# Attention scores: the keys' low parts as two products of 64 rows, and transpositions taken in pairs

## The chip, the cores and the metric

The kernel runs on one core of a Trainium2 chip. The metric is the device time of one execution in microseconds (us). A profile is one execution recorded by the hardware profiler; its instructions stand at microseconds from the start of the span.

## What is computed

One layer of an encoder on 1024 tokens of width 1024: a norm and a projection, three mixers, a gated sum of the three, and a layer of 16 experts. The change lies in the third mixer, attention with 8 query heads of 64 columns on 2 key and value heads:

```python
def block(qb):
    s = jnp.einsum('bkgqd,bksd->bkgqs', qb, k_t).astype(jnp.float32)
    pr = jax.nn.softmax(s, axis=-1).astype(dt)
    return jnp.einsum('bkgqs,bksd->bkgqd', pr, v_t)
```

Queries and keys are normed and rotated before that, and everything is float32.

## The kernel before

TensorE (PE) multiplies in a rounded format, so every operand is split into a high part (rounded) and a low part (what the rounding left), and a product is summed from two or three products of parts. PE's order in attention is written out by hand, ScalarE (ACT), VectorE (DVE), GpSimd (POOL) and SyncE (SP, which issues most DMAs) are ordered by a scheduler that places an instruction where its own model of time says it can start. Tiles come from pools with a fixed number of buffers, and a pool that opens takes over room of one that has closed; its first writers then wait for the last users of that room.

`attention(g)` (L897) stands between the recurrent mixer (`gates_and_chain`, lines up to L894) and `mixers_to_experts` (L1041), whose first part, `phase3` (L1077), multiplies the three mixers' outputs with their branch weights. It goes like this:

- Keys (L906 to L915): for each of the 2 key heads a high part `kh` and a low part `kl`. The head's 64 rows stand twice in the 128 partitions, so that the same keys meet whatever lies in either half of a query tile.
- Queries, `queries(b)` (L927 to L937), for two heads at a time: the high part of a head's 64 rows goes to one half `a` of the partitions of a tile, the low part to the other half `o`. One product with 128 rows then sums (high + low) times the keys. ACT makes the high part, DVE (b = 0, 1) or POOL (b = 2, 3) the low one.
- Scores, `scores(u, t)` (L944): attention is cut into 16 units (a head and half of the tokens), a unit into 4 tiles of 128 queries. A tile's scores against 1024 keys are 4 products of 128 rows by 512 columns (L954 with `kh`, L955 with `kl`, for either half of the keys), 64 tiles in all. DVE takes the row's maximum (`mx`, L958), ACT the exponential with its sum (`P`, L961).
- `turned(u, kt)` (L966): the exponentials of 128 keys are turned by 4 transpositions on PE (L971) into one PSUM tile `pT` (3 buffers); ACT writes the high part `ph` (L980), DVE the low part `pl` (L981). The ninth turn of a unit (kt = 8) turns the reciprocal sums, read by L975 alone.
- `weighted(u, kt, part)` (L987): two products with the values (L995 with `ph`, L997 with `pl`) summed over the 8 key blocks in one PSUM tile `po` (1 buffer). After the eighth, ACT and DVE read it into `yc` (L1003), POOL multiplies by the reciprocals (L1004), and after every fourth unit POOL's queue stores `yc` (2 buffers) to DRAM (`d_yc`, L1008).

The order of PE is a list of slots, nine to a unit: the turn kt of unit u in slot 9u + kt, its products two slots later (`PO_LAG`, one more for the first), four scores to a unit, two slots apart. It is sorted by slot, and within a slot turns come first, then scores, then products.

`phase3` begins with `branch(0, ...)` (L1092): its left operands are the pooling mixer's output `d_yb`, four loads of 512 KB (`yraw`, 2 buffers, L1125), each split by ACT and DVE (L1083, L1084), and multiplied on PE (L263 to L265).

Of the kernel before, what the change touches and what calls it, by code (L numbers as in the profile page):

```python
# [9 lines left out]
F32 = mybir.dt.float32  # L10
F32R = mybir.dt.float32r
# [9 lines left out]
S = 1024  # L21
# [9 lines left out]
SC_LEAD, SC_STEP, MX_LAG, EX_LAG, PO_LAG, PO_EXTRA, Q_LEAD, P_BUFS, PH_BUFS = 11, 2, 0, 1, 2, 1, 16, 13, 5  # L31
# [865 lines left out]
def attention(g):  # L897
    nc, tc = g.nc, g.tc
    with ExitStack() as es:
        psa = es.enter_context(tc.tile_pool(name="psa", bufs=3, space=PSUM, reuse_waits="tile"))  # L900
        pso = es.enter_context(tc.tile_pool(name="pso", bufs=1, space=PSUM, reuse_waits="tile"))
        pss = es.enter_context(tc.tile_pool(name="pss", bufs=2, space=PSUM, reuse_waits="tile"))


        kh, kl = [], []
        for kv in range(2):  # L906

            k = g.W.tile("w_raw")
            for h in range(2):
                nc.sync.dma_start(k[h * 64:(h + 1) * 64], g.d_qk[4, kv * 64:(kv + 1) * 64])  # L910
            th, tl = g.tile4k(S, F32R), g.tile4k(S, F32R)
            nc.scalar.activation(th, k, AF.Copy)
            nc.vector.tensor_tensor(tl, k, th.bitcast(F32), op=ALU.subtract)
            kh.append(th)
            kl.append(tl)  # L915

        vr = g.tile4k()
        nc.sync.dma_start(vr, g.d_qk[5])
        vr = vr.rearrange("p (t h v) -> p t h v", t=8, h=2)
        vv = [g.tile4k(S, F32R).rearrange("p (t a v) -> p t a v", t=8, a=2) for _ in range(2)]  # L920
        for kv in range(2):
            nc.scalar.activation(vv[kv][:, :, 0], vr[:, :, kv], AF.Copy)
            nc.vector.tensor_tensor(vv[kv][:, :, 1], vr[:, :, kv], vv[kv].bitcast(F32)[:, :, 0], op=ALU.subtract)

        QS = {}

        def queries(b):  # L927
            eng = getattr(nc, ENG_Q[b])
            q = g.W.tile("w_raw")
            nc.sync.dma_start(q, g.d_qk[b])  # L930
            for h in range(2):
                a = slice(h * 64, h * 64 + 64)
                o = slice(64 - h * 64, 128 - h * 64)
                t = g.W.tile(("w_hi", "w_lo")[h])
                nc.scalar.activation(t[a], q[a], AF.Copy)
                eng.tensor_tensor(t[o], q[a], t.bitcast(F32)[a], op=ALU.subtract)
                QS[2 * b + h] = t  # L937

        atb = es.enter_context(tc.tile_pool(name="atb", bufs=1, reuse_waits="tile"))

        UNITS = [(h, half) for h in range(8) for half in range(2)]
        P, PO, YC = {}, {}, {}

        def scores(u, t):  # L944

            h, half = UNITS[u]
            kv, q = h // 4, QS[h]
            if t == 0:
                P[u] = [], atb.tile([128, 4], F32, name="smx", bufs=4)
            qs = slice(half * 512 + t * 128, half * 512 + (t + 1) * 128)  # L950
            p = pss.tile([128, S], F32, name="sc", tag="sc")
            for n in range(2):
                ks = slice(n * 512, (n + 1) * 512)
                nc.tensor.matmul(p[:, ks], q[:, qs], kh[kv][:, ks], start=True, stop=False)  # L954
                nc.tensor.matmul(p[:, ks], q[:, qs], kl[kv][:, ks], start=False, stop=True)  # L955
            mx = atb.tile([128, 1], F32, name="mx", bufs=14)
            yield
            nc.vector.tensor_reduce(mx, p, op=ALU.max, axis=AX.X, negate=True)  # L958
            yield
            pt = atb.tile([128, S], F32, name="P", bufs=P_BUFS)  # L960
            nc.scalar.activation(pt, p, AF.Exp, bias=mx, accum_out=P[u][1][:, t:t + 1])  # L961
            P[u][0].append(pt)
            if t == 3:
                nc.vector.reciprocal(P[u][1], P[u][1])

        def turned(u, kt):  # L966

            p = psa.tile([128, 512], F32, name="pT", tag="sa")
            for t in range(4):
                a = P[u][0][t][:, kt * 128:(kt + 1) * 128] if kt < 8 else P[u][1][:, t:t + 1].to_broadcast([128, 128])  # L970
                nc.tensor.transpose(p[:, t * 128:(t + 1) * 128], a, g.ident)  # L971
            if kt == 8:
                rb = atb.tile([128, 512], F32, name="rb", bufs=2)
                r = head(u)
                nc.scalar.activation(rb[r], p[r], AF.Copy)  # L975
                P.pop(u)
                return rb[r]
            ph = atb.tile([128, 512], F32R, name="ph", bufs=PH_BUFS)
            pl = atb.tile([128, 512], F32R, name="pl", bufs=PH_BUFS)
            nc.scalar.activation(ph, p, AF.Copy)  # L980
            nc.vector.tensor_tensor(pl, p, ph.bitcast(F32), op=ALU.subtract)  # L981
            return ph, pl

        def head(u):
            return slice(UNITS[u][0] % 2 * 64, UNITS[u][0] % 2 * 64 + 64)

        def weighted(u, kt, part):  # L987

            h, half = UNITS[u]
            kv = h // 4  # L990
            if kt == 0:
                PO[u] = pso.tile([128, 512], F32, name="po", tag="po")
            po = PO[u]
            if kt < 8:
                nc.tensor.matmul(po, vv[kv][:, kt].rearrange("p a v -> p (a v)"), part[0], start=(kt == 0), stop=False,  # L995
                                 skip_group_check=True)
                nc.tensor.matmul(po[0:64], vv[kv][:, kt, 0], part[1], start=False, stop=(kt == 7), skip_group_check=True)  # L997
                return
            if u % 4 == 0:
                YC[0] = atb.tile([128, S], F32, name="yc", bufs=2)  # L1000
            yc = YC[0]
            y = yc[head(u), half * 512:(half + 1) * 512]
            last = [nc.scalar.activation(y, po[64:128], AF.Copy), nc.vector.tensor_add(y, y, po[0:64])]  # L1003
            nc.gpsimd.tensor_mul(y, y, part)  # L1004
            if u == W_AFTER:
                g.marks = [i.ins for i in last]
            if u % 4 == 3:
                nc.gpsimd.dma_start(g.d_yc[h // 2], yc)  # L1008

        E = mybir.EngineType  # L1010
        with ExitStack() as em:
            if ATT_MANUAL:
                em.enter_context(tc.manual_schedule(engines={getattr(E, e) for e in ATT_MANUAL}))
            nu = len(UNITS)

            todo = []
            for u in range(nu):
                for t in range(4):
                    s = u * 9 + t * SC_STEP - SC_LEAD
                    st = scores(u, t)  # L1020
                    todo += [(s, 2, st), (s + MX_LAG, 3, st), (s + EX_LAG, 4, st)]
                for kt in range(9):
                    i = u * 9 + kt
                    todo.append((i, 1, ("T", u, kt)))
                    todo.append((i + PO_LAG + (PO_EXTRA if kt == 0 else 0), 5, ("O", u, kt)))
            for b in range(4):
                todo.append((b * 36 - SC_LEAD - Q_LEAD, 0, b))
            todo.sort(key=lambda x: x[:2])
            parts = {}
            for i, k, x in todo:  # L1030
                if k == 0:
                    queries(x)
                elif k in (2, 3, 4):
                    next(x, None)
                elif k == 1:
                    parts[x[1:]] = turned(*x[1:])
                else:
                    weighted(*x[1:], parts.pop(x[1:]))
# [620 lines left out]
def hybrid_trunk_kernel(ctx: ExitStack, tc: tile.TileContext, names, *args):  # L1659
# [34 lines left out]
    if True:  # L1694
        with ExitStack() as ea:
            g.early = ea.enter_context(tc.tile_pool(name="early", bufs=1, reuse_waits="tile"))
            g.Dt = g.early.tile([64, 2, 8, NCH], F32, name="Dt")
            tp = ea.enter_context(tc.tile_pool(name="t4", bufs=1, reuse_waits="tile"))
            g.tile4k = lambda n=S, dt=F32: tp.tile([128, 1056], dt, name="tmp", tag="tmp", bufs=N_TMP)[:, :n]
            g.W = Weights(g, ea.enter_context(tc.tile_pool(name="wst", bufs=1, reuse_waits="tile")), W_RAW, 2)  # L1700
            phase1(g)
            attention(g)
        mixers_to_experts(g)
# [43 lines left out]
```

## Time and profile before

| | us |
|---|---|
| three runs, median (lowest to highest) | 2044.52 (2040.13 to 2051.64) |
| profiled execution, its time | 2044.28 |
| its span, first to last instruction | 2042.0 |
| attention, first score on PE to last product on PE | 895.5 to 1090.5 |

The profile gives each engine's busy time, a timeline of its instructions with what ended an idle time ahead of them, waits by pair of instructions, and for DMAs the issue and, for POOL's queue, the landing. A matmul's shape stands as rows*columns of the weights, so `128*128` is a full one, `64*128` one of 64 rows and `128*64` one of 64 columns. A matmul's recorded length overlaps the next one, so it is the distance of starts that tells what one costs PE. "issue" names an idle time that nothing in the profile explains.

### The profile page before, as it was taken

What the parts mean: (1) busy time and instruction counts of PE and PEld (TensorE: products, weight loads), DVE (VectorE), ACT (ScalarE), POOL (GpSimd) and SP (SyncE); (2) the same over time, 40 slices, a digit from 0 to 9 for tenths busy, and PEclk for the clock granted to TensorE, in tenths of its full rate; (3) what the DMA queues carried; (4) which work ended last, traced back from release to release, by engine and by line L of the source; (5) the groups of instructions that cost most, each with busy time, mean ns of one, the idle gap of its engine ahead of it and who ended that gap; (6) DMA issues with size and microseconds to landing.
All of it is one profiled execution on the core that took longest, in us unless ns stands there. A gap on an engine that the chain in (4) does not pass through costs nothing. (4 is left out here: it accounts for less than half of the span.)

```text
span 2042.0 us, 30594 instructions
## 1 busy us (share of the span) xinstructions
PE 1895.8 (93%) x11324; PEld 1531.2 (75%) x11324; DVE 1439.5 (70%) x2265; ACT 1042.8 (51%) x1539; POOL 566.1 (28%) x668
## 2 busy tenths in 40 slices
PE   6999999999989999989998989996779999999994
PEld 5878878778868888867776768874568888777883
DVE  6464465755165456668987893668969999888896
ACT  4454345531213321248885221334658888777784
POOL 2211112463156344302111575435211010100111
PEclk9999989999989999999998999997989999999997
DMA  5225353584299999920004644367879999995994
GB/s 158 62 73 138 100 149 95 152 196 111 86 189 171 167 207 196 201 104 32 11 12 159 220 132 164 144 220 285 310 261 382 395 387 400 389 374 182 342 385 171
DMA packets 394185, 403.80 MB, mean 198 GB/s; under 512 B 235111, under 2 KB 313525, under 8 KB 394037
## 3 DMA queue, kind: packets, MB, share of 16 engines
q1 hardware_dynamic: 385252, 373.00, 59.2%
q0 software_dynamic: 8784, 28.86, 5.2%
q8 instruction: 89, 1.46, 0.3%
q14 instruction: 60, 0.48, 0.1%
HBM read 325.73 MB, written 76.06 MB: 197 GB/s over the span
## 5 line engine op out<-in xcount | busy, mean ns | idle before, releaser
L263 PE MATMUL mm<-hn_hi,w_hi 128*128 128x512 f32 x592 | 234.5, 396 | 1.4 <-ACT w_hi L257 1.4
L264 PE MATMUL mm<-hn_lo,w_hi 128*128 128x512 f32 x592 | 235.3, 397 | 0.0
L265 PE MATMUL mm<-hn_hi,w_lo 128*128 128x512 f32 x592 | 233.5, 395 | 0.0
L258 DVE TENSOR_TENSOR w_lo<-w_raw,w_hi 128x1024 fp32r<-128x1024 f32 x56 | 76.1, 1358 | 122.6 <-ACT w_hi L257 122.6
L263 PEld LDWEIGHTS mm<-hn_hi,w_hi 128*128 128x128 f32 x592 | 112.0, 189 | 27.4 <-issue 3.2
L1482 DVE TENSOR_TENSOR lo<-wh,hi 128x1024 fp32r<-128x1024 f32 x103 | 123.2, 1220 | 10.9 <-ACT hi L1473 9.9
L264 PEld LDWEIGHTS mm<-hn_lo,w_hi 128*128 128x128 f32 x592 | 112.0, 189 | 24.8 <-issue 2.6
L265 PEld LDWEIGHTS mm<-hn_hi,w_lo 128*128 128x128 f32 x592 | 112.2, 190 | 24.3 <-issue 1.2
L1482 DVE TENSOR_TENSOR lo<-wl,hi 128x1024 fp32r<-128x1024 f32 x102 | 122.1, 1225 | 9.7 <-ACT hi L1473 8.7
L257 ACT ACTIVATE w_hi<-w_raw 128x1024 fp32r<-128x1024 f32 x56 | 59.1, 1057 | 131.2 <-PE mm L264 99.7
L1473 ACT ACTIVATE hi<-wh 128x1024 fp32r<-128x1024 f32 x104 | 109.3, 1060 | 32.8 <-PE py L265 16.6
L1473 ACT ACTIVATE hi<-wl 128x1024 fp32r<-128x1024 f32 x104 | 107.6, 1057 | 22.4 <-PE pg L265 10.1
L263 PE MATMUL pg<-hi,xgh 128*128 128x512 f32 x256 | 104.2, 407 | 7.7 <-ACT xgh L1502 7.7
L826 ACT ACTIVATE sv<-pu 32x128 f32<-32x128 f32 x128 | 33.8, 269 | 148.1 <-DVE sv L828 123.1
L832 PEld LDWEIGHTS pf<-sv,ot 128*96 128x96 f32 x1024 | 98.2, 172 | 10.5 <-DVE sv L828 4.2
L265 PE MATMUL pg<-hi,xgl 128*128 128x512 f32 x256 | 102.6, 401 | 3.3 <-DVE xgl L1503 3.2
L264 PE MATMUL pu<-lo,xgh 128*128 128x512 f32 x256 | 102.1, 399 | 1.6 <-POOL lo L1480 1.5
L264 PE MATMUL pg<-lo,xgh 128*128 128x512 f32 x256 | 103.0, 402 | 0.5 <-POOL lo L1480 0.5
L832 PE MATMUL pf<-sv,ot 128*96 128x64 f32 x1024 | 99.3, 256 | 3.2 <-DVE sv L828 2.9
L263 PE MATMUL pu<-hi,xgh 128*128 128x512 f32 x256 | 100.8, 394 | 1.5 <-DVE hid L1523 1.5
L264 PE MATMUL py<-lo,hidh 128*128 128x512 f32 x240 | 96.4, 402 | 5.9 <-DVE lo L1482 5.6
L265 PE MATMUL pu<-hi,xgl 128*128 128x512 f32 x256 | 100.0, 391 | 0.0
(422 smaller groups left out, 5147.5 us busy)
## 6 DMA issues: line engine op xcount, KB each, us to landing
w_raw<-in_w_in_dram SPq DMA_DIRECT2D x49, 512.0 KB
wh<-in_exp_up_dram SPq DMA_DIRECT2D x23, 1024.0 KB
wl<-in_exp_up_dram SPq DMA_DIRECT2D x22, 1024.0 KB
wl<-in_exp_down_dram SPq DMA_DIRECT2D x20, 1024.0 KB
wh<-in_exp_down_dram SPq DMA_DIRECT2D x20, 1024.0 KB
mg<-in_exp_gate_dram SPq DMA_DIRECT2D x19, 1024.0 KB
yr<-in_exp_up_dram SPq DMA_DIRECT2D x14, 1024.0 KB
yr<-in_exp_gate_dram SPq DMA_DIRECT2D x13, 1024.0 KB
```

Source lines behind the costliest of these rows:

```text
L257: nc.scalar.activation(hi, raw, AF.Copy)
L258: nc.vector.tensor_tensor(lo, raw, hi.bitcast(F32), op=ALU.subtract)
L263: nc.tensor.matmul(out, ah, bh, start=start, stop=False)
L264: nc.tensor.matmul(out, ah, bl, start=False, stop=False)
L265: nc.tensor.matmul(out, al, bh, start=False, stop=stop)
L826: nc.scalar.activation(sv[96:128, q::4, :], pu[r], AF.Copy)
L832: nc.tensor.matmul(pf[0:96, q, :], ot[:, q, 0:96], sv[:, q, :], start=True, stop=True)
L1473: nc.scalar.activation(hi, raw[:, j], AF.Copy)
L1482: nc.vector.tensor_tensor(lo, raw[:, j], hi.bitcast(F32), op=ALU.subtract)
```

## The change

The products with the keys' low parts take 64 rows where they took 128: for the first 512 keys the rows `a`, with the query's high part that lies there, for the other 512 keys the rows `o`, with a copy `q2` of that high part, made by POOL. The product of low part with low part is left out. Two turns are put into one even slot, one behind the other, and the products with values follow in pairs.

```diff
@@ queries(b), in the loop over the two heads
                 nc.scalar.activation(t[a], q[a], AF.Copy)
                 eng.tensor_tensor(t[o], q[a], t.bitcast(F32)[a], op=ALU.subtract)
-                QS[2 * b + h] = t
+
+                t2 = atb.tile([128, S], F32R, name="q2", bufs=4)
+                nc.gpsimd.tensor_copy(t2[o], t.bitcast(F32)[a])
+                QS[2 * b + h] = t, t2, a, o
@@ scores(u, t)
             for n in range(2):
                 ks = slice(n * 512, (n + 1) * 512)
                 nc.tensor.matmul(p[:, ks], q[:, qs], kh[kv][:, ks], start=True, stop=False)
-                nc.tensor.matmul(p[:, ks], q[:, qs], kl[kv][:, ks], start=False, stop=True)
+
+            nc.tensor.matmul(p[:, :512], q[a, qs], kl[kv][a, :512], start=False, stop=True)
+            nc.tensor.matmul(p[:, 512:], q2[o, qs], kl[kv][o, 512:], start=False, stop=True)
@@ the list of slots
+            at = 0
...
                 for kt in range(9):
                     i = u * 9 + kt
-                    todo.append((i, 1, ("T", u, kt)))
-                    todo.append((i + PO_LAG + (PO_EXTRA if kt == 0 else 0), 5, ("O", u, kt)))
+
+                    todo.append((i // 2 * 2, 1, ("T", u, kt)))
+                    at = max(at, i // 2 * 2 + PO_LAG + (PO_EXTRA if kt == 0 else 0))
+                    todo.append((at, 5, ("O", u, kt)))
```

In the changed kernel the lines are L958 (scores, high), L960 and L961 (the two of 64 rows), L977 (transpositions), L1001 and L1003 (products with values), L939 (the copy), L1134 (`yraw`), L1111 (`sg`), L1014 (the store of `yc`).

PE, in the middle of attention. `sc` are scores, `pT` transpositions, `po` products with values. Before:

```order
L954 MATMUL sc<-tmp,w_hi 128x512
L955 MATMUL sc<-tmp,w_hi 128x512
L954 MATMUL sc<-tmp,w_hi 128x512
L955 MATMUL sc<-tmp,w_hi 128x512
L995 MATMUL po<-ph,tmp 128x512
L997 MATMUL po<-pl,tmp 64x512
L971 MATMUL pT<-ident,P 128x128 x8
```

After, in the same stretch:

```order
L958 MATMUL sc<-tmp,w_hi 128x512 x2
L960 MATMUL sc<-tmp,w_hi 128x512
L961 MATMUL sc<-tmp,q_9132 128x512
L1001 MATMUL po<-ph,tmp 128x512
L1003 MATMUL po<-pl,tmp 64x512
L1001 MATMUL po<-ph,tmp 128x512
L1003 MATMUL po<-pl,tmp 64x512
L977 MATMUL pT<-ident,P 128x128 x8
```

The count of matmuls is the same; the two with low keys now stand side by side at the end of a score, and behind the 64 scores stand 37 times a product with values, 23 times transpositions and 4 times the next score (at the very start, where scores run ahead).

SP, from the last store of the stage ahead of attention into `phase3`; the names in brackets are the semaphores that an issue waits for, by engine or DMA queue (DMASW are POOL's queues). Before:

```order
L725 DMA d_sig<-gate 128x512 [waits Activation_49]
L1125 DMA yraw<-d_yb 128x1024 [waits DMASW5_49,DMASW4_49,DMASW6_49,DMASW3_49,DMASW7_49,DMASW2_49,DMAHW5_49,DMASW1_49,DMASW0_49]
L1125 DMA yraw<-d_yb 128x1024 [waits DMASW7_49,DMAHW6_49,DMASW1_49,PE_49]
L1102 DMA sg<-d_sig 128x1024 [waits DMAHW7_49,DMAHW4_49]
L1102 DMA sg<-d_sig 128x1024 [waits DMAHW0_49]
L1102 DMA sg<-d_sig 128x1024 [waits DMAHW1_49]
L240 DMA w_raw<-in_w_branch_pool_dram 128x4x256 [waits DMAHW2_49,DVE_49]
L240 DMA w_raw<-in_w_branch_pool_dram 128x4x256 [waits DMAHW3_49,DVE_49]
L1135 DMA lnw<-in_rwkv_ln_w_dram 128x512 [waits PE_49]
```

After:

```order
L240 DMA w_raw<-in_w_branch_pool_dram 128x4x256 [waits DMAHW5_49,DMAHW1_49,DVE_49]
L240 DMA w_raw<-in_w_branch_pool_dram 128x4x256 [waits DMAHW6_49,DMAHW2_49,DVE_49]
L1134 DMA yraw<-d_yb 128x1024 [waits DMASW4_49,DMASW5_49,DMASW3_49,DMASW6_49,DMASW2_49,DMASW7_49,DMASW1_49,DMAHW7_49,DMASW0_49,Pool_49]
L1134 DMA yraw<-d_yb 128x1024 [waits DMAHW0_49,DMASW7_49,PE_49]
L1144 DMA lnw<-in_rwkv_ln_w_dram 128x512 [waits DVE_49,PE_49]
L1145 DMA lnb<-in_rwkv_ln_b_dram 128x512
L1148 DMA sgd<-d_sg 128x1024 [waits DMAHW4_49,DVE_49,PE_49]
L1153 DMA yf<-d_y 128x512 [waits DMAHW5_49]
L1156 DMA vt<-d_v 128x512 [waits DMAHW6_49,PE_49]
L1111 DMA sg<-d_sig 128x1024 [waits DMAHW7_49]
```

The first two loads of `yraw` and the three of `sg`, which stood ahead of everything that waits for attention, now stand in it: `q2` takes four buffers of the pool `atb`, the tiles behind it move up, and `yraw`'s first buffer comes to lie where `yc` lies. In the built program the count that `yraw`'s new wait for POOL asks for is that of attention's last multiplication (L1010 of the last unit), and the one on DMASW3 that of the last store of `yc` (L1014).

## Rows read from the trace of the kernel before

**Rows 1.** Windows, ten of 10 us inside attention, summed: busy us of each engine.
```profile
sum 100.00, PE 100.00 PEld 79.52 DVE 89.87 ACT 88.20 POOL 18.15; mean PE 10.00 PEld 7.95 DVE 8.99 ACT 8.82 POOL 1.82
```

**Rows 2.** Timeline of PE in attention: start us, us, engine, line, operation, tiles, shape, count.
```profile
985.84 0.40 PE L995 MATMUL po<-ph,tmp 128*128 128x512 f32 x1
986.07 0.39 PE L997 MATMUL po<-pl,tmp 128*64 128x512 f32 x1
986.30 0.60 PE L971 MATMUL pT<-ident,P 128*128 128x128 f32 x4
986.66 0.47 PE L995 MATMUL po<-ph,tmp 128*128 128x512 f32 x1
986.97 0.40 PE L997 MATMUL po<-pl,tmp 128*64 128x512 f32 x1
```

**Rows 3.** The same view around a product of 64 rows, second stage.
```profile
240.41 0.39 PE L438 MATMUL sm<-xw,w2p 128*128 128x512 f32 x1
240.73 0.49 PE L439 MATMUL sm<-xw,w2p 64*128 64x512 f32 x1
241.15 0.50 PE L264 MATMUL mm<-hn_lo,w_hi 128*128 128x512 f32 x1
241.49 0.40 PE L265 MATMUL mm<-hn_hi,w_lo 128*128 128x512 f32 x1
```

**Rows 4.** Waits of line L439 (all products of 64 rows by 512 columns): cause, us, times.
```profile
  issue: 10.2, 32
```

**Rows 5.** The PE timeline again, a product of 64 rows ahead of eight transpositions.
```profile
243.22 0.50 PE L439 MATMUL sm<-xa,a2p 64*128 64x512 f32 x1
243.65 1.09 PE L603 MATMUL sm<-ident,tmp 128*128 128x128 f32 x8
244.50 0.47 PE L265 MATMUL mm<-hn_hi,w_lo 128*128 128x512 f32 x1
```

**Rows 6.** The same view, eight transpositions in a row in attention.
```profile
992.63 1.04 PE L971 MATMUL pT<-ident,P 128*128 128x128 f32 x8
993.42 0.48 PE L954 MATMUL sc<-tmp,w_hi 128*128 128x512 f32 x1
```

**Rows 7.** PE timeline, products of half the rows and columns: windows 167.460:167.465, then 167.465:167.475.
```profile
167.36 0.33 PE L572 MATMUL sm<-ra,kb 64*64 64x64 f32 x3
...
167.36 0.33 PE L572 MATMUL sm<-ra,kb 64*64 64x64 f32 x4
```

**Rows 8.** Timeline of DVE, two low parts and the next one behind them.
```profile
1019.54 1.87 DVE L981 TENSOR_TENSOR pl<-pT,ph 128x512 fp32r<-128x512 f32 x3
```

**Rows 9.** Timeline at the end of attention, PE, then POOL, then ACT.
```profile
1090.50 0.41 PE L997 MATMUL po<-pl,tmp 128*64 128x512 f32 x1
1092.67 1.44 PE L263 MATMUL mm<-wh,w_hi 128*128 128x512 f32 x4 [1.76 <-ACT wh L1083]
...
1093.92 0.56 POOL L1008 DMA_DIRECT2D d_yc<-yc  x1 [0.30 <-POOL yc L1004]
...
1106.36 1.06 ACT L1083 ACTIVATE wh<-yraw 128x1024 fp32r<-128x1024 f32 x1 [2.19 <-DMA yraw<-d_yb]
```

**Rows 10.** Timeline of SyncE's queue (SPq): DMA issues, ahead of and behind attention.
```profile
896.10 0.84 SPq L1125 DMA_DIRECT2D yraw<-d_yb  x2
...
1102.02 0.38 SPq L1125 DMA_DIRECT2D yraw<-d_yb  x1
```

**Rows 11.** Line L1008, the four stores of an attention output.
```profile
DMA to landing us min/median/max: 3.0/3.0/7.6
```

**Rows 12.** Windows behind attention: busy us, clock, DMA share, GB/s.
```profile
1105.00:1110.00 5.00, 3.38 (x9) 2.36 (x8) 4.87 (x8) 1.69 (x2) 2.43 (x3) 0.71 0.99 338
...
1160.00:1200.00 40.00, 32.59 (x131) 24.71 (x130) 39.83 (x82) 7.53 (x13) 26.46 (x18) 0.91 0.46 146
```

**Rows 13.** Groups by form, POOL, whole program.
```profile
L162 POOL COPY half<-krn 128x512 f32<-128x512 f32 x8 | 5.5, 721 | 97.2 <-DVE krn L208 57.9 <-ACT att_in L407 39.3
```

More of the change, by code (lines that the diff above doesn't have):

```diff
@@ L946, in scores @@
             h, half = UNITS[u]
-            kv, q = h // 4, QS[h]
+            kv = h // 4
+            q, q2, a, o = QS[h]
             if t == 0:
```

## The prediction

> **What bounds the kernel now.** The profiled execution took 2044.28 us, 2.3 of it outside its span of 2042.0; the median of the three runs, 2044.52, is the same within 0.25, so the sums below start from 2044.3. A measurement here tells a kernel from this one at about 0.5%, which is 10.2 us: under 2034.3 is faster, over 2054.7 slower.
>
> I looked first at the windows inside attention. Over ten of 10 us PE is busy 100 of 100 us, DVE 89.87, ACT 88.20, POOL 18.15 [rows 1]. A busy PE may still be an idle one, because its records overlap, so I looked next at the distances of starts in its timeline. A product of 512 columns starts 0.23 after the one ahead of it, also behind one that uses 64 columns of the weights; four transpositions take 0.36, and the first product behind them is followed after 0.31, not 0.23 [rows 2]. There is no gap in these figures to be filled. In attention, then, what lengthens PE's list lengthens the kernel one for one, and what only comes earlier on another engine brings nothing. How far the engines behind PE would follow a shorter list is seen in the same row: DVE has 10% to spare, ACT 12%.
>
> Then I looked for anything in this program that resembles the new products: 64 rows by 512 columns. The second stage has 32 of them, L439, each between full products. The start of one stands 0.32 behind the product ahead of it, the next product stands 0.42 behind that, and the one after another 0.34 [rows 3]. The weight load of L439 sat idle 10.2 us in 32 times, 0.32 each, for no reason the profile names [rows 4]: it isn't one bad case. So a visit to 64 rows costs PE at both doors, and for products that use only half of the columns, nothing of the kind is seen [rows 2].
>
> **The score products.** Today a score is 4 x 0.23 = 0.92. After the change: 0.23 from the first high product to the second; 0.32 to the first product of 64 rows; the second one stands beside it, in the other half of the rows. For its distance I use the products of 64 rows by 64 columns: in one stretch three records and four records fill the same 0.33 us, so the fourth starts with the third [rows 7]; I take 0.01. Then 0.42 to whatever follows, and 0.34 - 0.23 = 0.11 more behind that, if it is a product: 0.23 + 0.32 + 0.01 + 0.42 + 0.11 = 1.09, or +0.17 a score. If eight transpositions follow, 0.43 stands for 0.42 and the transpositions take 0.85 [rows 5] against 0.79 in attention now [rows 6], so 0.23 + 0.32 + 0.01 + 0.43 + 0.06 = 1.05, or +0.13. The order gives 41 scores of the first kind (37 ahead of a product with values, 4 ahead of a score) and 23 of the second: 41 x 0.17 + 23 x 0.13 = 7.0 + 3.0 = **+10.0**. Its ends are the rivals' cases below: the two not beside each other, and no price at the doors. The product of low with low that is left out takes no time with it, because a product's time goes by columns and the column count of each matmul stays.
>
> On this point the trace speaks against a simple gain. The Trainium skill, "TensorEngine Tiling (Array Packing)", Theoretical Speedup, gives up to 2x for a dimension of at most 64; by that alone a score would take 3 x 0.23 = 0.69, and 64 scores would save an estimated 14.7 us; the mechanism is a rival below. The same page, Key Properties, says that changing the tiling mode, and not just the tile, drains the engine; by that rule the sum stays as above, and the trace agrees: 0.32 ahead of L439 and 0.42 behind it [rows 3]. But the page lists 128x64 as a configuration of its own, and there the trace shows no drain: 0.23 into it [rows 2].
>
> **Pairs of turns.** Eight transpositions and the longer step behind them take 0.79 + 0.08 = 0.87, two times four take 2 x (0.36 + 0.08) = 0.88 [rows 2, 6]. Over 64 pairs that is 0.6 us, which I put at 0. The cost may lie on DVE. The two low parts of a pair are made one behind the other, 1.87 / 3 = 0.62 apart [rows 8], while PE would use them 2 x 0.23 = 0.46 apart: up to 0.16 late for each of 64 pairs, 10 us, if nothing else stood between. The other end is 0: products lag the turns by two slots, with scores between, and that covers a lateness of 0.16 where DVE isn't also at a maximum of a score. I take **+2**, nearer to 0, because DVE has a tenth of its time free [rows 1], and the pairs come with two scores of cover each.
>
> **POOL's copies.** Eight copies of 64x1024. A copy of 128x512 took 0.72 [rows 13], half the elements in a lane; I estimate 1.44 each. POOL is idle four fifths of attention [rows 1], and all but the first copy have units of lead, so 0; the upper end is the one copy ahead of the first score, 1.4. A queue behind them: POOL's low parts for the later heads, released just as far ahead.
>
> **The handover to the next stage.** This is the part that the diff doesn't show. In the order the first `yraw` load now waits for attention's last POOL multiplication and the last store of `yc`. Today both first loads are issued at 896.10, as attention begins [rows 10], and the first product of the next stage starts 1092.67 - 1090.50 = 2.2 after attention's last [rows 9]. After the change: store issued 3.4 after that last product [rows 9], landed 3.0 later where the queues are calm [rows 11], the load until its use 1106.36 - 1102.02 = 4.3 [rows 9, 10], ACT's split 1.1 [rows 9]: 11.8, so 9.6 later. But PE is not dense there today either: the fourth load reaches ACT only 1106.36 - 1090.50 = 15.9 behind the last product [rows 9], with the DMA engines 0.99 busy at 338 GB/s [rows 12]. What is new for those engines is at least two loads of 512 KB, 1.05 MB / 338 GB/s = 3.1. The cost so lies between 3.1 and 9.6 at this place; in the stretch 1160 to 1200 PE is idle 7.4 us with DVE full [rows 12], so a part or all of it could be lost there if DVE catches up, but DVE is full, which speaks against it. I take the middle, **+6**, with ends 0 and 10. SP is queued behind the waiting load: `lnw`, `lnb`, `sgd` and the three `sg`, whose users stand behind the first products of the stage.
>
> **The sum.** 10 + 2 + 0 + 6 = 18: 2044.3 + 18 = **2062**. With the small ends of pairs and handover 2054.3, with both large 2074; its own range is 2055 to 2071.
>
> **Rivals.**
>
> *Not side by side.* The second product of 64 rows starts 0.23 behind the first. For it: L439 never has a partner, and the trace shows it for 64 columns alone [rows 7]. Against it: the two share no rows, whatever their columns. 64 x 0.22 = 14 more: 2076. The same would be the time if the change does not do what it says.
>
> *The doors are free here (the other side).* In the second stage L439's weights and operands come fresh from other engines; in attention they lie ready long before. Then a score is 3 x 0.23 + 0.01 = 0.70, and 64 x 0.22 = 14 are saved: 2030, or 2038 with the 8 of the other terms. It decides at a price of 0.22 for both doors together; the doors cost (0.32 - 0.23) + (0.42 - 0.23) + 0.11 = 0.39 in the second stage [rows 3]. Against it: all 32 idled, for "issue" and not for data [rows 4].
>
> *The handover and the pairs are hidden.* The scores alone cost: 2044.3 + 10 = 2054.
>
> **How the numbers follow.** Forecast 0.60; not side by side 0.15; free doors 0.10; hidden 0.15. Slower by over 0.5%: 0.60 + 0.15, and little of the hidden case, which lies just under the bound: 0.76. Faster: of the free doors the half without the other terms, 0.06. Same: 0.18. The range leaves out the free doors and the far ends of the serial case: 2050 to 2077.
>
> **What would show it.** Right: L960 starts 0.32 behind the second L958, L961 within 0.01 of it, the next 0.42 behind; the weight load of L960 idle for "issue"; PE still 10 of 10 in the windows of attention; the first L263 of the next stage 11 to 12 behind the last L1003; the last `yc` store landing ahead of the first `yraw` load. Wrong: L961 0.2 behind L960 (serial), L960 0.23 behind L958 (free doors), idle time of PE for `pl` over 5 us (pairs cost more), or the end of the kernel no later than attention's end is (handover hidden).

## The result and the profile after

The changed kernel took 2067.46 us, the median of four runs (2062.53 to 2072.56), against 2044.89 for the kernel before: a ratio of 1.0112, 95% interval 1.0093 to 1.0132. It is slower, by 22.6 us; the forecast was 2062, range 2050 to 2077.

The profiled execution took 2064.15, its span is 2062.4, 20.4 longer than before. Along PE's timeline that is: attention begins 1.1 earlier, takes 207.7 instead of 195.0 from its first score to its last product (+12.7), the gap to the next stage is 11.6 instead of 2.2 (+9.4), 1.5 of which is caught up before the experts begin, and 0.8 is added behind. So two places carry it, attention and the handover.

A score in attention, in PE's timeline of the changed kernel (columns as in [rows 2]; L958 high keys, L960 and L961 the two of 64 rows):

```profile
983.58 0.71 PE L958 MATMUL sc<-tmp,w_lo 128*128 128x512 f32 x2
984.22 0.50 PE L960 MATMUL sc<-tmp,w_lo 64*128 64x512 f32 x1
984.23 0.50 PE L961 MATMUL sc<-tmp,q 64*128 64x512 f32 x1
984.65 0.50 PE L1001 MATMUL po<-ph,tmp 128*128 128x512 f32 x1
985.00 0.40 PE L1003 MATMUL po<-pl,tmp 128*64 128x512 f32 x1
985.23 1.04 PE L977 MATMUL pT<-ident,P 128*128 128x128 f32 x8
```

L961 starts 0.01 behind L960, L1001 0.42 behind that, L1003 0.35 behind L1001, and transpositions then at the usual 0.23. The longer steps into and out of the products of 64 rows are called the doors below, and one stay between a step in and a step out is a visit. Over all 64 scores the mean step from the second high product to L960 is 0.33, that from L960 to L961 0.003. The idle time of the weight load ahead of L960, whose like in the kernel before are [rows 4]:

```profile
  issue: 23.9, 64
```

0.37 each, and 64 of 64. In twelve windows of 10 us in attention (950 to 1070) PE is no longer busy throughout, as it was in [rows 1]:

```profile
sum 120.00, PE 117.85 PEld 79.92 DVE 102.47 ACT 98.14 POOL 20.08; mean PE 9.82 PEld 6.66 DVE 8.54 ACT 8.18 POOL 1.67
```

The end of attention (timelines of PE, ACT, POOL and SyncE's queue), to be read beside [rows 9, 10]:

```profile
1102.11 0.41 PE L1003 MATMUL po<-pl,tmp 128*64 128x512 f32 x1
1113.66 2.08 PE L263 MATMUL mm<-wh,w_hi 128*128 128x512 f32 x4 [11.14 <-ACT wh L1092]
...
1112.56 1.06 ACT L1092 ACTIVATE wh<-yraw 128x1024 fp32r<-128x1024 f32 x1 [9.41 <-DMA yraw<-d_yb]
...
1105.50 0.56 POOL L1014 DMA_DIRECT2D d_yc<-yc  x1 [0.30 <-POOL yc L1010]
...
1108.66 0.81 SPq L1134 DMA_DIRECT2D yraw<-d_yb  x2
```

The store of `yc` is issued 3.4 behind the last product; the loads of `yraw` go out 3.2 behind the store, as soon as it has landed (the four stores of `yc` land 2.9 to 3.2 behind their issue), and the first of them is split 3.9 later. The next stage's first product starts 11.55 behind attention's last; the prediction had 11.8.

### The profile page after: what moved, and what is told of

The parts are those of the page before. It is cut to its first block, busy times and chain, and to the rows that moved or that the text cites. A ratio compares the mean times of both kernels' runs of the same rounds, so it can differ in the third digit from the quotient of the medians.

```text
span 2062.4 us, 30580 instructions
## 1 busy us (share of the span) xinstructions
PE 1899.6 (92%) x11324; PEld 1514.9 (73%) x11324; DVE 1444.5 (70%) x2265; ACT 1041.6 (51%) x1539; POOL 571.7 (28%) x676
## 5 line engine op out<-in xcount | busy, mean ns | idle before, releaser
L1553 POOL DMA_INDIRECT d_x<-yo,idx_t x14 | 22.2, 1586 | 280.8 <-ACT yo L1545 280.5
```

The source lines that it names most:

```text
L1553: nc.gpsimd.indirect_dma_start(out=dst, out_offset=bass.IndirectOffsetOnAxis(ap=chosen(e)[1], axis=0), in_=rows, in_offset=None, compute_o ...
```

## The experiments

Eleven kernels were run. Their numbers together; "unit" is the mean length of a unit in the steady part, from the first transposition of the fourth unit to that of the fourteenth, divided by ten, and "to experts" goes from attention's last product to the first transposition of the experts' stage. Attention, unit, gap and the last column are of one profiled execution each, the ratio is to the kernel before on the same chip.

| kernel | ratio (95%) | attention | unit | gap | to experts |
|---|---|---|---|---|---|
| before | | 195.0 | 11.49 | 2.2 | 304.2 |
| the change | 1.0112 (1.0093 to 1.0132) | 207.7 | 12.39 | 11.6 | 312.1 |
| single_turns | 1.0081 (1.0056 to 1.0106) | 203.2 | 11.96 | 11.5 | 310.3 |
| q2_on_top | 1.0076 (1.0057 to 1.0095) | 214.2 | 12.39 | 2.2 | 307.2 |
| same_half | 1.0189 (1.0170 to 1.0208) | 220.3 | 13.10 | 11.4 | 312.5 |
| pairs_alone | 1.0036 (1.0019 to 1.0054) | 206.0 | 12.16 | 2.2 | 307.2 |
| copies_alone | 1.0028 (1.0016 to 1.0040) | 196.7 | 11.50 | 11.6 | 312.0 |
| pairs_in_unit | 1.0081 (1.0059 to 1.0102) | 213.7 | 12.85 | 2.2 | 302.0 |
| low_beside | 1.0022 (1.0009 to 1.0035) | 196.4 | 11.44 | 2.2 | 308.4 |
| low_same | 1.0102 (1.0085 to 1.0120) | 206.9 | 12.28 | 2.1 | 307.5 |
| low_unit | 1.0044 (1.0026 to 1.0061) | 202.9 | 11.99 | 2.2 | 305.3 |
| low_half | 0.9974 (0.9963 to 0.9986) | 187.5 | 10.92 | 2.1 | 306.7 |
| low_full | 1.0027 (1.0006 to 1.0048) | 197.3 | 11.50 | 2.2 | 303.9 |

Single executions of one kernel lie up to 16 us apart, so the whole time of one profile decides little; the unit, a mean over ten, is the steadier reading.

### The three terms, one at a time

**single_turns**: the change without the pairs.

```diff
-                    todo.append((i // 2 * 2, 1, ("T", u, kt)))
-                    at = max(at, i // 2 * 2 + PO_LAG + (PO_EXTRA if kt == 0 else 0))
-                    todo.append((at, 5, ("O", u, kt)))
+                    todo.append((i, 1, ("T", u, kt)))
+                    todo.append((i + PO_LAG + (PO_EXTRA if kt == 0 else 0), 5, ("O", u, kt)))
```

> The change without the pairs of turns: one turn to a slot, as before, with the scores in products of 64 rows. Theory (doors 10, pairs about 3, handover about 8): attention from first score to last product takes 205 us, against 207.7 in the changed kernel and 195.0 before; PE hardly waits for low parts; the gap to the next stage stays near 11.6; time 2064. Rival one (pairs cost nothing, all 12.7 us are the doors): attention 207.7, time 2067. Rival two (the pairs are the larger part): attention 200 or less, time under 2060.

Attention 203.2 and the gap 11.5: the scores alone make attention 8.2 longer, 0.47 a unit. The pairs bring the other 4.5, 0.44 a unit. That is nearer to the theory than to either rival; the pairs cost somewhat more than its 3. By the medians the change stands 0.31% above this kernel, some 6 us, with intervals that overlap.

The steps in PE's timeline account for the 0.47. The doors take 0.59 a unit: 0.24 in the scores' own steps, 0.29 in the step behind the first product after them, 0.06 in transpositions. And 0.12 comes back. In the kernel before, the first product of every unit starts late behind its transpositions, since `po` is still being read into `yc`: here 0.51 behind the first of four transpositions and not 0.36, or 0.20 behind the last and not 0.03.

```profile
960.16 0.60 PE L971 MATMUL pT<-ident,P 128*128 128x128 f32 x4
960.67 0.50 PE L995 MATMUL po<-ph,tmp 128*128 128x512 f32 x1
...
PEld po L995 <- DVE yc L1003: 0.8, 5, 0.2
```

The last line is from the waits of 960 to 1075: us, times, longest. In single_turns such a product always starts 0.03 behind the last transposition, and PE is busy 120.00 of 120 us in the twelve windows; so what PE idles in the changed kernel's windows comes with the pairs.

**pairs_alone**: the kernel before with the change's slot list and nothing else (the diff above, turned round).

> The kernel before with the turns in pairs and nothing else. Theory: PE loses about 3 us in attention waiting for high and low parts and for the one output tile, attention 198, gap to the next stage 2.2, time 2047.5. Rival (the pairs cost nothing): attention 195.0, time 2044.5. Rival two (fewer changes between transpositions and products are a gain): attention 193, time 2042.

All three theories missed: 12.16 a unit and 206.0; by the ratio the kernel is 7 us (4 to 11) slower, its profiled execution being the slowest of its eight. Without the products of 64 rows the pairs cost 0.67 a unit, 10.7 over 16, more than beside them: the two costs don't add. That fits a PE which, held up at its doors, gives the other engines the time that the pairs want: from 950 to 1070 PE is idle 4.56 us here and 2.15 in the change. Where the time goes stands in PE's timeline; these are the only three waits over 0.15 us of two units in the steady part:

```profile
991.69 0.40 PE L955 MATMUL sc<-tmp,w_lo 128*128 128x512 f32 x1
992.32 0.49 PE L995 MATMUL po<-ph,tmp 128*128 128x512 f32 x1 [0.24 <-DVE yc L1003]
...
998.79 0.60 PE L971 MATMUL pT<-ident,smx 128*128 128x128 f32 x4
999.80 0.66 PE L971 MATMUL pT<-ident,P 128*128 128x128 f32 x4 [0.41 <-DVE pl L981]
...
1000.76 0.40 PE L995 MATMUL po<-ph,tmp 128*128 128x512 f32 x1
1001.53 0.44 PE L997 MATMUL po<-pl,tmp 128*64 128x512 f32 x1 [0.37 <-DVE pl L981]
```

They all lie where one unit meets the next: a product waits for the one output tile `po` to be read into `yc` (a step of 0.63, not 0.23), a turn for DVE to give back a `pT` tile (1.01, not 0.36), a low product for DVE's `pl` (0.77, not 0.23): 1.6 together, against a measured 1.34 for two units. From 960 to 1075 the waits for `po` and `pl` come back in every two units; that for `pT` stands there twice, one of the two inside a unit:

```profile
PE po L997 <- DVE pl L981: 1.8, 5, 0.4
PE po L995 <- DVE yc L1003: 1.6, 5, 0.4
PE pT L971 <- DVE pl L981: 0.6, 2, 0.4
```

So pairs inside a unit wait little. Nor is it shown that DVE has too much to do at the border: just ahead of the late low parts it stands idle.

```profile
998.57 0.18 DVE L964 RECIPROCAL smx<-smx 128x4 f32<-128x4 f32 x1 [1.40 <-ACT P L961]
999.05 0.69 DVE L981 TENSOR_TENSOR pl<-pT,ph 128x512 fp32r<-128x512 f32 x1 [0.31 <-ACT ph L980]
```

It waits for the unit's last exponential, because the reciprocal stands ahead of the low parts in its queue; ACT makes the high part only behind that exponential, and a maximum stands between the two low parts. No run changed that order.

**pairs_in_unit**: so a pair across two units might be the cause. The kernel before with pairs inside a unit:

```diff
-                    todo.append((i, 1, ("T", u, kt)))
-                    todo.append((i + PO_LAG + (PO_EXTRA if kt == 0 else 0), 5, ("O", u, kt)))
+                    i = u * 9 + kt // 2 * 2
+                    todo.append((i, 1, ("T", u, kt)))
+                    at = max(at, i + PO_LAG + (PO_EXTRA if kt == 0 else 0))
+                    todo.append((at, 5, ("O", u, kt)))
```

> The kernel before with turns in pairs inside a unit, the ninth turn alone, so that no pair lies across two units. Theory (the cost of the pairs alone, 12.16 us a unit against 11.49 in the steady part, is three stalls at every second border of two units: products waiting for the one output tile, a turn and a low product waiting for DVE): 11.5 to 11.7 a unit, attention 195 to 199, time 2046 to 2050. Rival (DVE's second low part of a pair is late everywhere, borders or not): still 12.1 to 12.2 a unit, attention 206, time 2056.

The theory fell, and its rival too: units take 11.5 and 14.2 in turn. PE's waits from 960 to 1075:

```profile
PE pT L971 <- DVE pl L981: 8.1, 5, 1.7
PE po L997 <- DVE pl L981: 3.1, 4, 0.8
```

At a border PE now has the ninth turn, four products with values, a pair, a score and the next pair. At one border of two, that second pair waits 1.7 for DVE to free `pT`; at the other, a product waits 0.8 for a low part. So the cost of the pairs lies in the bunch of work at a border, and pairing inside a unit makes the bunch worse. That DVE is too slow for it isn't shown. Ahead of the 1.7 it is idle twice, for ACT's part of `yc` and for a score whose maximum comes first in its queue:

```profile
994.22 0.68 DVE L1003 TENSOR_TENSOR yc<-yc,po 64x512 f32<-64x512 f32 x1 [0.50 <-ACT yc L1003]
995.39 1.22 DVE L958 TENSOR_REDUCE mx<-sc 128x1 f32<-128x1024 f32 x1 [0.49 <-PE sc L955]
996.65 1.89 DVE L981 TENSOR_TENSOR pl<-pT,ph 128x512 fp32r<-128x512 f32 x3
```

Which piece of a border's work (`yc`, the reciprocal, the maxima, their order) costs it, no run took apart.

**copies_alone**: the kernel before, with the copies made and not used.

```diff
+                t2 = atb.tile([128, S], F32R, name="q2", bufs=4)
+                nc.gpsimd.tensor_copy(t2[o], t.bitcast(F32)[a])
                 QS[2 * b + h] = t
```

> The kernel before with POOL's eight copies q2 added and read by nobody, so that only the room in the pool and POOL's work are changed. Theory (the move of yraw's buffer is a cost by itself): attention 195 to 196 us, the gap to the next stage 11.5 instead of 2.2, the experts start some 5 to 6 later, time 2052 against 2046.5 for the kernel before in the same job. Rival (the next stage catches it up): the gap 11.5 and the time within 2 us of the kernel before.

```profile
1093.33 0.41 PE L999 MATMUL po<-pl,tmp 128*64 128x512 f32 x1
1104.91 1.65 PE L263 MATMUL mm<-wh,w_hi 128*128 128x512 f32 x3 [11.18 <-ACT wh L1085]
```

The theory holds: attention's unit is unchanged (11.50 against 11.49), the gap is 11.6, and the kernel is 1.0028 of the one before, 5.7 us (3.3 to 8.2). The four buffers of a tile that nobody reads are enough for it. Four profiles with the gap reach the experts 310.3 to 312.5 behind attention, those without it 302.0 to 308.4: about 6 by their means, 311.7 and 305.8.

**q2_on_top**: the change, with the copies in a pool of their own behind `atb`.

```diff
+        atq = es.enter_context(tc.tile_pool(name="atq", bufs=1, reuse_waits="tile"))
...
-                t2 = atb.tile([128, S], F32R, name="q2", bufs=4)
+                t2 = atq.tile([128, S], F32R, name="q2", bufs=4)
```

> The changed kernel with the copies q2 in a pool of their own behind attention's other tiles, so that the first yraw loads wait for an early score and not for the last output of attention. Theory (the gap of 11.6 us comes from these loads alone): attention stays at 207.7, the gap to the next stage falls to 2 to 3 us, time 8 us lower than the changed kernel, 2059 (2057 to 2061). Rival (the gap is caught up later anyway, and the loss behind attention has another cause): gap 2 to 3, time within 2 us of the changed kernel, 2066 to 2068.

Half of it came. The gap is 2.2 again, and the experts start 4.9 earlier behind attention; but attention is 214.2. Its steady unit, 12.39, is that of the change; what was lost lies in its first units, where a score waits for a copy:

```profile
PE sc L962 <- POOL q L939: 3.6, 1, 3.6
```

The copies now lie over other tiles of the stage before and are late: POOL's first one waits for a store of that stage and starts at 901.74, in the change at 893.06.

```profile
901.74 1.03 POOL L939 CAST q<-w_hi 64x1024 fp32r<-64x1024 f32 x1 [35.12 <-DMA d_y<-y]
```

The ratio, 1.0076, is below that of the change, but the intervals touch. Moving the buffer moved the collision.

### Whether two products really stand side by side

**same_half**: the second low product in the rows of the first.

```diff
-            nc.tensor.matmul(p[:, 512:], q2[o, qs], kl[kv][o, 512:], start=False, stop=True)
+            nc.tensor.matmul(p[:, 512:], q[a, qs], kl[kv][a, 512:], start=False, stop=True)
```

> The changed kernel with both low products of a score in the same half of the rows, so that they cannot stand side by side; the copy q2 is made and not read. Theory (side by side is real and worth a whole product): the second starts 0.22 us behind the first, attention 207.7 + 64 x 0.22 = 221.8, time 2081. Rival (the starts 0.003 apart are of the record alone, and the engine takes them one after the other anyway): attention 207.7, time 2067.

```profile
985.82 0.49 PE L960 MATMUL sc<-tmp,w_lo 64*128 64x512 f32 x1
986.15 0.39 PE L961 MATMUL sc<-tmp,w_lo 64*128 64x512 f32 x1
986.47 0.50 PE L1001 MATMUL po<-ph,tmp 128*128 128x512 f32 x1
```

The second starts 0.33 behind the first, and the next 0.32 behind that, where the change has 0.01 and 0.42: 0.22 more a score. The unit is 0.71 longer (0.18 a score) and attention 12.6, near the theory's 14. Side by side is real and gives 0.22 by the steps; the doors take (0.33 - 0.23) + (0.42 - 0.23) + (0.35 - 0.23) = 0.41 by the steps of the change.

**low_beside, low_same, low_full**: is it the halves, their rows, or only these scores? The products with the low parts of the exponentials use 64 columns of the weights, with no door [rows 2]. Here they are taken two at a time, in bfloat16, in the two halves of the columns (`low_beside`) or both in the same half (`low_same`):

```diff
-                nc.tensor.matmul(po[0:64], vv[kv][:, kt, 0], part[1], start=False, stop=(kt == 7), skip_group_check=True)
-                return
+                low = LOW.pop(u, [])
+                low.append((kt, part[1]))
+                if kt % 2 == 0:
+                    LOW[u] = low
+                    return
+                for n, (k1, pl) in enumerate(low):
+                    nc.tensor.matmul(po[n * 64:n * 64 + 64], vb[:, k1, kv], pl, start=False, stop=(kt == 7), skip_group_check=True)
+                return
...
-            pl = atb.tile([128, 512], F32R, name="pl", bufs=PH_BUFS)
+            pl = atb.tile([128, 512], BF16, name="pl", bufs=PH_BUFS)
```

`vb` is a copy of the values in bfloat16; `low_same` writes both to `po[0:64]`; `low_full` keeps the old order and gives the low product 128 columns, 64 of them zero.

> Another way to use half of the array: the kernel before, with the low parts of the exponentials in bfloat16 and the products of two of them with the values taken side by side in the two halves of the columns, one into rows 0 to 63 of the output tile and one into rows 64 to 127, which are added anyway. Turns as before. Theory (two column halves work at the same time, and this mode has no price at the doors): 64 x 0.22 = 14 us less, 10.6 us a unit where DVE needs some 10.3, attention 181 to 184, time 2033 to 2036. Rival (two products that need all rows go one behind the other): starts 0.23 apart, attention 195, time 2046. Rival two (the doors cost here as they do for half of the rows): attention over 200, time over 2051.

> The control of the run with low products side by side: the same bfloat16 low parts in the same order, but both of a pair into rows 0 to 63, the same half of the columns. All theories: starts 0.23 apart, 11.5 us a unit, attention 195, time within 2 us of the kernel before.

> The kernel before with the low parts of the exponentials in bfloat16 and their products with all 128 columns of weights, of which 64 are zero: the type changes between neighbours on PE, the mode of the array does not. Theory (it is the mode that has doors, not the type): starts 0.23 apart, 11.5 us a unit, attention 195, time within 3 us of the kernel before. Rival (the change of type drains, the half columns had nothing to do with it): 0.32 ahead of each low product and 0.34 behind, 128 visits at 0.2 to 0.25, attention over 220, time over 2068.

In PE's timeline, of `low_beside`, `low_same` and `low_full` in turn:

```profile
988.41 0.40 PE L997 MATMUL po<-ph,tmp 128*128 128x512 f32 x1
988.73 0.41 PE L1005 MATMUL po<-pl,vb 128*64 128x512 bf16 x2
989.07 0.65 PE L973 MATMUL pT<-ident,smx 128*128 128x128 f32 x4
989.48 0.48 PE L997 MATMUL po<-ph,tmp 128*128 128x512 f32 x1
```

```profile
991.22 0.39 PE L997 MATMUL po<-ph,tmp 128*128 128x512 f32 x1
991.54 0.62 PE L1005 MATMUL po<-pl,vb 128*64 128x512 bf16 x2
992.09 0.65 PE L973 MATMUL pT<-ident,smx 128*128 128x128 f32 x4
```

```profile
987.89 0.40 PE L998 MATMUL po<-ph,tmp 128*128 128x512 f32 x1
988.13 0.39 PE L1000 MATMUL po<-pl,vb 128*128 128x512 bf16 x1
988.36 0.60 PE L974 MATMUL pT<-ident,smx 128*128 128x128 f32 x4
```

Two low products take 0.41 of record in the two halves and 0.62 in one: they work side by side here too, and the units of 11.44 and 12.28 differ by 0.84, 0.21 for each of four pairs. But the step into them is 0.32 and that out of them 0.34, and the transpositions behind take 0.41, not 0.36; doors, where products of the same shape in the kernel before have none. So `low_beside` comes out at a unit of 11.44 where 10.6 was expected, and `low_same`, expected to be the kernel before, is 0.79 a unit longer: 0.20 for each of its four visits. The short wait of 0.12 a unit at `po`, which the kernel before has (single_turns), is gone in both; with it a visit costs 0.23 in either, (0.79 + 0.12) / 4 and (0.84 + 0.12 - 0.05) / 4. `low_full` has steps of 0.24 and 0.23 in these rows and a unit of 11.50: a change of type alone has no doors. Whether bfloat16 and 64 columns together have them, and 64 columns in float32 not, is what the rows suggest and no run took apart. Its ratio is nevertheless above 1, barely; attention's unit gives no reason.

**low_unit, low_half**: if the doors are paid by the visit, a longer visit pays. The list `low` is emptied at eight parts, or at four, with 12 and 8 buffers of `pl`:

```diff
+                if len(low) == 4:
+                    for n, (k1, pl) in enumerate(LOW.pop(u)):
+                        o = n % 2 * 64
+                        nc.tensor.matmul(po[o:o + 64], vb[:, k1, kv], pl, start=False, stop=(kt == 7), skip_group_check=True)
```

> The run with low products side by side in the two halves of the columns, but all eight low products of a unit kept to its end and made in four pairs in a row, one visit to the mode of half columns in a unit. There a visit cost about 0.25 us at its doors and a pair gave back 0.21. Theory (the doors are paid by the visit, not by the product): 4 x 0.21 - 0.25 = 0.59 us less a unit, 10.9 against 11.49 before in the steady part, attention 186 to 189, time 9 us under the kernel before, ratio 0.994 to 0.997. Rival (the doors are paid by each pair): 11.45 a unit, ratio 1.000 to 1.003. Rival two (the one output tile, held longer at the end of a unit, becomes the wait): over 11.5 a unit.

> The same with two visits in a unit, each of four low products in two pairs. Theory (doors by the visit): 0.84 - 0.50 = 0.34 us less a unit, 11.15, attention 190, ratio 0.997. Rival (by the pair): 11.45 a unit. If the output tile is the wait in the run with one visit, this one is the faster of the two.

```profile
991.72 0.40 PE L997 MATMUL po<-ph,tmp 128*128 128x512 f32 x1
992.05 0.62 PE L1004 MATMUL po<-pl,vb 128*64 128x512 bf16 x4
992.60 1.09 PE L973 MATMUL pT<-ident,P 128*128 128x128 f32 x8
...
sum 40.00, PE 40.00 PEld 30.67 DVE 37.77 ACT 37.98 POOL 10.51; mean PE 10.00 PEld 7.67 DVE 9.44 ACT 9.49 POOL 2.63
```

```profile
995.68 0.40 PE L997 MATMUL po<-ph,tmp 128*128 128x512 f32 x1
996.01 1.05 PE L1004 MATMUL po<-pl,vb 128*64 128x512 bf16 x8
...
PE pT L973 <- DVE pl L983: 10.9, 10, 1.2
```

Two products take 0.41 of record, four 0.62, eight 1.05: 0.21 for each further pair (0.21 to 0.24 by the starts), and the step of 0.33 into them once a visit. Doors are paid by the visit. `low_half` has a unit of 10.92, better than the 11.15 worked out, and is faster than both kernels: 0.9974 (0.9963 to 0.9986). About half of what it is better by is the wait of 0.12 at `po`, which is gone here too; the rest is a price of (4 x 0.21 + 0.12 - 0.57) / 2 = 0.19 a visit in place of 0.25. PE is busy throughout there, DVE 37.77 of 40. `low_unit` loses more than it wins, to the second rival in another form: once a unit, PE waits for DVE to give back a `pT` tile, 10.9 in 115 us. That DVE is late there because `po` is read late, behind eight products, fits (ACT waits for them ten times in that stretch, 4.9 us in all), and wasn't tried.

## Why the prediction was right

**What bounds.** Right: PE's list decided in attention, to the point that a product placed beside another is worth its 0.22 (same_half, low_same). But "There is no gap in these figures to be filled" missed the 0.12 a unit at `po`, and with the pairs PE waits.

**The score products, +10.** The steps came as forecast from L439: 0.33 in (0.32), 0.003 between (0.01), 0.42 out (0.42), 0.35 behind (0.34). The term was 10.0; single_turns makes attention 8.2 longer, and 16 x 0.47 = 7.5 in the steady part. By the steps the doors cost 0.59 a unit, 9.4 over 16, near the 10; the 1.9 less is the wait at `po` that PE had before and no longer has, which the sum left out. "4 x 0.23 = 0.92" for a score of the kernel before is too low, 1.01 in the steady part, since the first product behind transpositions takes 0.32; that stays after the change, and so cancels in the difference.

**Not side by side, free doors.** Both rivals fell at L961 and at L960 in the first profile, and same_half put the size on the first: 12.6 in attention against 14.

**Pairs of turns, +2.** This is the step that failed, in its reason and its size. The prediction put it as "up to 0.16 late for each of 64 pairs", the second low part made 0.62 behind the first and used 0.46 behind it; but pairs inside a unit hardly wait. Most waits stand at the borders of units, for `po`, `pl` and at times `pT`. And the size is 4.5 (0.44 a unit, 7.0 over 16) beside the doors and 10.7 without them: not 2, and without the doors at the end that was called far. There are 72 pairs, and 56 of them have two low parts; the count of 64 is a small matter. "DVE has a tenth of its time free" was read from 100 us, and a mean says nothing of what happens in the 2 us around a border, where DVE is idle and late at once. Two of the prediction's own signs pointed here: PE is busy 117.85 of 120 us and not throughout, and over the whole of attention it idles 5.1 us for `pl` (2.9 in the kernel before), just over the 5 that was to mean that pairs cost more. What sets the lateness at a border stays open.

**The handover, +6.** Right in mechanism and size: 11.55 from product to product against 11.8, and 5.7 us by copies_alone, 7.9 in the change's own profile up to the experts. Part of the 9.4 is caught up, as was assumed between the bounds; how much is rough, since kernels without the gap reach the experts up to 6.4 apart.

**The sum.** 10 + 2 + 6 = 18 against 22.6; the profiles give 8.2 + 4.5 + 7.9 = 20.6. Two errors, a score term that left out the wait it takes away and pairs too cheap, nearly cancelled in attention (12 forecast, 12.7 measured), so the good total is in part luck.

**The sentence on half columns.** The prediction set it against a rule of the Trainium skill, "TensorEngine Tiling (Array Packing)", Key Properties, that products with 64 columns showed no drain in and out. The comparison misled: low_same and low_beside, of the same recorded shape, do show it, and low_full excludes the change of type by itself. That page of the Trainium skill says that changing the mode drains the engine, and the traces of low_same and low_beside agree, 0.20 to 0.23 a visit. Why the old products with 64 columns pay nothing, these runs don't show; the shape in the record doesn't tell.

## What to carry to other kernels

Splitting the array pays by the visit: count the visits, take the price of going in and out from the nearest products in your own trace, and put enough pairs into a visit (with halves of the columns four products, not two) before it is worth anything. The same for halves of the rows, the low products of several scores in one visit, was not run. A new tile in a pool can cost more than the work done in it: look in the order of the queue for loads that now wait for something late. And a stage-wide mean of an engine's free time does not cover a bunch: look at the places where two units meet.

## What was not expected of the hardware

Two products that need all 128 rows, but go to different halves of the columns, work side by side as those in different halves of the rows do, as low_beside's theory had it; what it did not have is that this, too, has doors. Inside a visit a further pair starts 0.21 to 0.24 behind the one ahead of it, where in low_same a single product takes 0.24. Products whose record says 64 columns can be with or without doors. And a PE that is slowed by one cost seems to absorb part of another: the pairs cost 0.67 us a unit in a kernel with a dense PE and 0.44 in one with doors.
